# A hybrid decoder layer on one core: sample rows' output product on array quarters, the sample recurrence paused in each head's first group, weights on ScalarE's queue

## The chip, the cores and the metric

The kernel runs on one core of a Trainium2 chip. The core has TensorE (PE, a 128x128 array of multipliers; its weight loads are listed apart as PEld), VectorE (DVE), ScalarE (ACT), GpSimd (POOL) and SyncE (SP). SP computes nothing and issues most of the DMA transfers, in the order of its queue; ScalarE has a DMA queue too. The metric is the device time of one execution in microseconds. The times given are the median of several runs.

## The reference

One layer of a decoder works on 1024 prompt rows and on 32 sample rows (8 sequences of 4 new tokens), each of 1024 numbers:

```
h = x @ w_in                                     # 9344 columns
y_r = rwkv_mix(shifted columns, state)           # RWKV-7: 8 heads of 64, a recurrence over the tokens
y_a = merged dilated attention (3 groups x 4 heads x 128), softmax over the groups, times silu(gate)
mix = sigmoid(g_r) * (y_r @ w_oa) + sigmoid(g_a) * (y_a @ w_ob)
y   = layer_norm(ALPHA * x + mix @ w_out) * ln_g + ln_b
```

The outputs are `y` of the prompt and of the sample rows, the new keys and values, the new states of the recurrence and the last shifted row. Everything is fp32.

## The kernel before, in words

Tokens lie along columns: 1024 prompt tokens and 32 sample tokens make 1056 columns, worked in three chunks of 352 (`CH`). Large products are made of three products each (`mm3`, L171): operands are split into a high part and a rest (`hi`, `lo`, of type fp32r), and `hi*hi`, `lo*hi` and `hi*lo` are added up in PSUM. One chunk of one block of 128 output columns takes twelve products for 512 rows of the contraction.

The order of the work is written as a sequence of Python calls. A planner then lays out each engine's queue from it: by the written order first, but an instruction that is not ready in its model of the times can be passed by a later one. In stage one the order of TensorE is fixed by hand (`run_streams`); from there on the planner lays it out. Instructions given to `tc.keep_in_program_order` stay behind all that was written before them on their engine.

**Stage one** projects the shifted columns and the gates and runs the recurrence of the prompt. The change does not touch it.

**Attention** goes over four heads `h` and, in each, three groups `g`; n = 3h + g numbers these twelve steps. Each projects values, keys and queries (18 slots of twelve products) and between the slots works off a list `steps` of small closures that belong to the group before (`interleave`). So the closing work of head h is done among the projections of the next head's first group (g = 0). This closing work is of two kinds. `s_values` (`sv`) finishes the sample rows' attention: `pv0`, `pv1` and `pv2` multiply probabilities by cached values (L1093, on quarters of the array: the four sets of 32 output rows of the array, chosen by the partitions of the output), `pv2` then scales the result into `son` (L1113), and `out` transposes `son` on TensorE (L1118). `merge` (`me`) combines the three groups of the prompt's attention: `combine` computes weights and writes them to memory (`cd`), they come back spread over all partitions (`cb`, L1172), and `weight(0)`, `weight(1)`, `weight(2)` (L1177, L1180) and `last` (L1183) multiply and add 128x1024 tiles on VectorE.

The **sample recurrence** (`rec_step`, L760 to L767) is 16 steps of eight VectorE operations on 128x512 elements, 128 operations in all, with one GpSimd operation a step (L757). `interleave` calls `rec_some` after each slot, for one operation at a time, 18 a group. They are kept in program order. `rec_out` (L781 to L806), called at n = 10, stores the state, sends the outputs `oo` through memory (`od`, L782; back as `og` in tile `rtm`, L784), normalizes them on VectorE, transposes them (L798) and stores them for branch one.

**Branches.** `branch(0)` multiplies y_r by `w_oa`, `branch(1)` y_a by `w_ob`: 24 chunks each, eight blocks `d_` of three. Each chunk's gate `gt` (176 KB) is loaded by SP from `gd`, and VectorE multiplies PSUM by it: L1269 in branch one (in text: branch one is `b = 0`), L1266 in branch two, where GpSimd adds the result to `mix` (L1267). The first eight chunks of branch one run among the closing work of head 3. Beside branch two the rows of `w_out` are loaded into `xt` (three buffers, 512 KB each) and split into `wh` and `wl`.

**The last stage** (L1305) works off nine row blocks: eight of 128 prompt rows and one of the 32 sample rows. Each makes 48 products with 512 columns (L1323), adds the input (L1324), takes statistics (L1325, L1327), and normalizes: 704 columns (`CUT`) on VectorE, the other 320 with GpSimd's help.

Of the kernel before, what the change touches and what calls it, by code (L numbers as in the profile page):

```python
# [18 lines left out]
P = 128  # L19
D = 1024  # L20
# [25 lines left out]
def _constants():  # L46
# [17 lines left out]
    cst2 = np.concatenate([prev, cur, m3], 1)  # L64
# [18 lines left out]
def tile_layer(ctx: ExitStack, tc: tile.TileContext, A: dict, O: list):  # L83
# [72 lines left out]
    def load_w(src, n=4):  # L156
        raw = mk(wpool, [P, n, P], "wraw", 2)
        SP.dma_start(raw[:], src)
# [573 lines left out]
    SP.dma_start(cst2[:], A["cst2"])  # L732
# [325 lines left out]
    def s_values(h, Sa, sm):  # L1058
# [48 lines left out]
        def pv2():  # L1107
# [4 lines left out]
            for s_ in range(2):  # L1112
                V.tensor_scalar(on[:, s_], st["po"][s_][:, 0:P], sm[:, 5 + s_ : 6 + s_], None, ALU.mult)  # L1113
# [93 lines left out]
    for h in range(4):  # L1207
# [5 lines left out]
        for g in range(3):  # L1213
# [39 lines left out]
    def branch(b, hi, lo, w, mix):  # L1253
        cols = lambda d_: load_w(w[0, :, d_ * P : (d_ + 1) * P].rearrange("(k p) c -> p k c", p=P))
        ahead = cols(0)
        for d_ in range(8):
            wd, ahead = ahead, cols(d_ + 1) if d_ < 7 else None
            for c in range(3):
# [3 lines left out]
                gt = mk(stash, [P, CH], "gt", 3)  # L1262
# [15 lines left out]
    products = branch(0, yh, yl, A["w_oa"], mix)  # L1278
# [6 lines left out]
    for _ in products:  # L1285
        pass
# [3 lines left out]
    for n, _ in enumerate(branch(1, ah, al, A["w_ob"], mix)):  # L1290
        if n % 3 == 0:
            k = n // 3
# [7 lines left out]
    x_rows = lambda i: A["x_prompt"][0, i * P : (i + 1) * P, :] if i < 8 else A["x_sample"].rearrange("b t d -> (b t) d")  # L1300
    y_rows = lambda i: O[0][0, i * P : (i + 1) * P, :] if i < 8 else O[1].rearrange("b t d -> (b t) d")
    eps = mk(op, [P, 1], "eps")
    V.memset(eps[:], 16.0 * LN_EPS)
    CUT = 704
    for i in range(9):  # L1305
        n = P if i < 8 else NS
        sl = slice(i * P, i * P + n)
        mh, ml_ = (mk(op, [P, KT, P], t, 2, dt=F32R) for t in ("mh", "ml"))
        for h in range(2):
            k4 = slice(4 * h, 4 * h + 4)  # L1310
            split(mix[h][:, :, sl], mh[:, k4, 0:n], ml_[:, k4, 0:n])
        xt = mk(op, [P, D], "xt", 3)
        SP.dma_start(xt[0:n, :], x_rows(i))
        stt = mk(op, [P, 2, 6], "bst", 2)
# [48 lines left out]
```

## Time and profile before

| | |
|---|---|
| median of 3 runs | 1393.86 us (1392.2 to 1399.85) |
| profiled execution | 1398.63 us, its span 1396.8 us |
| TensorE products busy | 1354.3 us, 97% of the span |
| VectorE, ScalarE, GpSimd busy | 58%, 33%, 6% |
| mean granted TensorE clock | 0.993 |
| bytes moved by DMA | 151.29 MB, 108 GB/s on average |

The profile is one execution. Its span runs from the first to the last instruction on the core; the execution's own time is 1.8 us longer. In the timelines a row has the start and the length in us, the engine, the source line, the operation, output and inputs by name, the shapes, how many instructions were merged into the row, and in brackets the idle time before it with what ended it. A row of the waits gives engine, line, what was waited for, the total, how often, and the longest. In the groups the numbers behind the bar are busy us and mean ns of one, then the idle time before them.

### The profile page before, as it was taken

To read this page: it belongs to the slowest core of one execution; us is meant where nothing else is said; L and a number is where in the kernel's file an instruction comes from. 1 tells how busy PE (TensorE), PEld (TensorE's weight loads), DVE (VectorE), ACT (ScalarE), POOL (GpSimd) and SP (SyncE) were. 2 spreads that over 40 slices of the span, in tenths; PEclk is the share of its full clock that TensorE was granted. 3 is DMA by queue.
4 is the path that set the end of the run, shared out by engine and by line. 5 is a ranking of instruction groups with operands and counts; after the bars stand their busy time and mean duration, and the time that the engine had idled before them with its cause. 6 is when DMAs were issued, how large, how long until landed. Compare 5 with 4: busy or idle time off the path is not lost.

```text
span 1396.8 us, 25253 instructions
## 1 busy us (share of the span) xinstructions
PE 1354.3 (97%) x9765; PEld 1252.2 (90%) x9765; DVE 816.3 (58%) x2219; ACT 459.4 (33%) x1075; POOL 81.8 (6%) x92
## 2 busy tenths in 40 slices
PE   8999999999999999999999999999999999999997
PEld 7998989898988889999999899989998999898884
DVE  4358767586767767342555585548333524665675
ACT  4333434444344443422333223322323234132110
POOL 0000000000000000000000000000000000025122
PEclk9999999999999999999999999999999999999999
DMA  6212222312323233237544545555465556586121
GB/s 214 54 46 75 59 79 80 99 49 68 86 56 84 77 87 103 79 99 141 118 100 113 145 99 103 119 129 114 102 153 131 120 126 150 174 280 215 61 91 53
DMA packets 339742, 151.29 MB, mean 108 GB/s; under 512 B 188944, under 2 KB 329030, under 8 KB 339366
## 3 DMA queue, kind: packets, MB, share of 16 engines
q1 hardware_dynamic: 249190, 133.55, 35.0%
q10 hardware_dynamic: 90432, 16.13, 6.3%
q8 instruction: 77, 1.26, 0.4%
q14 instruction: 43, 0.35, 0.1%
HBM read 110.35 MB, written 38.97 MB: 107 GB/s over the span
## 4 chain that ended last, share of the span: by engine, by line
PE 76%; DVE 13%; DMA 6%; issue 2%; ACT 2%; POOL 0%; SPq 0%; DVEq 0%; ACTq 0%
PE pj L171 53%; PE pj L1323 7%; PE o L931 2%; PE s L894 2%; DVE tm L440 2%; DVE X L443 2%; DMA cb<-cd 2%; PE t L914 1%; PE s L1013 1%; PE sc L502 1%; DMA gt<-gd 1%; DVE wlo L162 1%; DMA cd<-nE 1%; PE g L369 1%; DVE st L510 1%
## 5 line engine op out<-in xcount | busy, mean ns | idle before, releaser
L171 PE MATMUL pj<-xhi,whi 128*128 128x352 f32 x1848 | 401.1, 338 | 4.3 <-DVE xlo L1269 2.0
L171 PE MATMUL pj<-xlo,whi 128*128 128x352 f32 x1848 | 384.0, 329 | 0.0
L171 PE MATMUL pj<-xhi,wlo 128*128 128x352 f32 x1848 | 382.8, 328 | 0.0
L171 PEld LDWEIGHTS pj<-xhi,whi 128*128 128x128 f32 x1848 | 304.8, 190 | 21.0 <-issue 10.4
L171 PEld LDWEIGHTS pj<-xhi,wlo 128*128 128x128 f32 x1848 | 309.3, 190 | 2.5 <-issue 0.8
L171 PEld LDWEIGHTS pj<-xlo,whi 128*128 128x128 f32 x1848 | 308.4, 190 | 2.9 <-issue 0.6
L162 DVE TENSOR_TENSOR wlo<-wraw,whi 128x512 fp32r<-128x512 f32 x162 | 113.1, 698 | 91.9 <-ACT whi L161 91.2
L161 ACT ACTIVATE whi<-wraw 128x512 fp32r<-128x512 f32 x162 | 100.7, 625 | 144.1 <-PE pj L171 71.5
L904 ACT ACTIVATE Sm<-Sm,nm 128x128 f32<-128x128 f32 (+1 forms) x96 | 42.4, 442 | 91.2 <-DVE nm L901 91.2
L510 DVE SCALAR_TENSOR_TENSOR st<-sc,E,SD 64x64 f32<-64x64 f32 x128 | 36.1, 282 | 47.3 <-PE sc L507 45.8
L1323 PE MATMUL pj<-wl,mh 128*128 128x512 f32 (+1 forms) x144 | 56.8, 394 | 0.0
L440 DVE TENSOR_TENSOR tm<-Y,X 128x60 f32<-128x60 f32 (+24 forms) x248 | 52.5, 212 | 6.3
L443 DVE TENSOR_TENSOR X<-X,tm 128x60 f32<-128x60 f32 (+24 forms) x248 | 51.9, 209 | 6.4
L896 DVE CUSTOM_DVE_ANT_0 Sm<-s,cst 128x128 f32<-128x128 f32 (+1 forms) x96 | 29.3, 346 | 41.4 <-PE s L894 41.3
L757 POOL TENSOR_TENSOR kvp<-vv,kv 128x512 f32<-128x512 f32 x16 | 21.1, 1324 | 406.4 <-DVE Ss L765 239.3
L493 ACT ACTIVATE SD<-st,E 128x128 f32<-128x128 f32 x64 | 25.6, 400 | 58.4 <-DVE st L510 58.4
L931 PE MATMUL o<-PT,Vt 128*128 128x128 f32 x280 | 38.7, 276 | 0.0
L819 ACT ACTIVATE k<-pj 128x352 f32<-128x352 f32 (+1 forms) x36 | 16.3, 454 | 66.2 <-PE pj L171 60.9
L894 PE MATMUL s<-k,q 128*128 128x128 f32 (+1 forms) x192 | 37.5, 325 | 0.0
L931 PEld LDWEIGHTS o<-PT,Vt 128*128 128x128 f32 x280 | 36.5, 191 | 0.4
L497 DVE TENSOR_TENSOR R<-sc,R 64x128 f32<-64x128 f32 x64 | 18.4, 288 | 30.4 <-PE sc L495 29.2
L502 PEld LDWEIGHTS sc<-R,AT 64*64 64x64 f32 x256 | 19.5, 133 | 18.1 <-DVE R L497 7.8
(295 smaller groups left out, 1753.9 us busy)
## 6 DMA issues: line engine op xcount, KB each, us to landing
wraw<-in_w_in_dram SPq DMA_DIRECT2D x146, 256.0 KB
gd<-zt SPq DMA_DIRECT2D x48, 176.0 KB
gt<-gd SPq DMA_DIRECT2D x48, 176.0 KB
vs<-bt ACTq DMA_DIRECT2D x48, 128.0 KB
kc<-in_cache_kv_g_dram SPq DMA_DIRECT2D x48, 128.0 KB
Vt<-vs ACTq DMA_DIRECT2D x12, 512.0 KB
cb<-cd SPq DMA_DIRECT2D x12, 512.0 KB
zd<-zt SPq DMA_DIRECT2D x24, 176.0 KB
```

The lines of the kernel that those rows point to most:

```text
L161: S.activation(hi[:], raw[:], AF.Copy)
L162: V.tensor_tensor(lo[:], raw[:], hi.bitcast(F32)[:], ALU.subtract)
L171: T.matmul(out, w[wi][:, n % 4, :], x[:, n % 4, :], start=first and n == 0, stop=last and n == 11)
L440: V.tensor_tensor(tm, Y[:, r : r + 1, r + 1 : 32].to_broadcast([P, m, n]), X[:, 0:m, r : r + 1].to_broadcast([P, m, n]), ALU.mult)
L443: V.tensor_tensor(X[:, 0:m, r + 1 : 32], X[:, 0:m, r + 1 : 32], tm, ALU.subtract)
L502: T.matmul(pu[u, 64 * e : 64 * e + 64], AT[u, e, c, u], R[u, 64 * e : 64 * e + 64], start=True, stop=True)
L510: V.scalar_tensor_tensor(S1[d, d], pS[d, d], E[d, c, 64:65], SD[d, d], ALU.mult, ALU.add)
L894: T.matmul(r, qT[:, i * P : (i + 1) * P], kT[:, keys[i][0] * P : keys[i][0] * P + n], start=True, stop=True)
L896: V.tensor_tensor_reduce(out=Sm[:, i, 0:n], in0=r, in1=m3 if g == 2 else m12[:, 256 - n : 256], scale=1.0, scalar=NEG, op0=ALU.add, op1=AL ...
L904: S.activation(Sm[:, i, 0:n], Sm[:, i, 0:n], AF.Exp, scale=SCALE, bias=nm[:, x : x + 1], accum_out=ml[:, g, 1, i : i + 1])
L931: T.matmul(po[:, (i % 4) * P : (i % 4 + 1) * P], st["Vt"][:, kb_, :], PT[:, n * P : (n + 1) * P], start=m == 0, stop=m == len(keys[i]) - 1,)
L1323: T.matmul(pb[0:n, :], a[:, k, 0:n], wk, start=x == 0, stop=x == len(prods) - 1)
```

## The change

1. **Sample rows.** The ninth row block of the last stage goes. Instead the sample rows' product with `w_out` is made beside branch two, in plain fp32 from the unsplit rows `raw` of `w_out`: for each of eight row blocks k of `w_out` one call of `sample_product(k)`, four products of 32 output rows and 256 columns, each on its own quarter of the array, added up in one PSUM tile `so`. It is called two blocks after `raw` was loaded, and k = 6 and 7 after the first row block of the last stage. `sample_norm` normalizes the result after the second row block: 32 rows of four quarters lie on 128 partitions, and two products with a constant matrix `quad` average over the four quarters. Its inputs are loaded late in branch two (`sample_loads`).
2. **Recurrence.** `rec_some` is called in groups with g > 0 only, where before it was called in all but the very first; what is left of the 128 operations is issued at n = 10, just ahead of `rec_out`.
3. **Closing work.** `son` is scaled on ScalarE instead of VectorE, and `out` comes behind `last` in the list.
4. **Weights of the branches** are issued on ScalarE's queue instead of SP's, two blocks ahead instead of one; `gt` has six buffers instead of three from the 19th chunk of branch one on.
5. **Last stage.** The normalization is written with fused operations, ScalarE does the scaling of the right part, GpSimd only one addition, `CUT` is 608, and in the last row block the second half of the columns is made in two products of 256 columns.

```diff
+    quad = np.where(i % 32 == j % 32, 0.25, 0.0)
+    cst2 = np.concatenate([prev, cur, m3, quad], 1)
...
-    def load_w(src, n=4):
+    def load_w(src, n=4, queue=SP):
         raw = mk(wpool, [P, n, P], "wraw", 2)
-        SP.dma_start(raw[:], src)
+        queue.dma_start(raw[:], src)
...
             for s_ in range(2):
-                V.tensor_scalar(on[:, s_], st["po"][s_][:, 0:P], sm[:, 5 + s_ : 6 + s_], None, ALU.mult)
+                S.activation(on[:, s_], st["po"][s_][:, 0:P], AF.Copy, scale=sm[:, 5 + s_ : 6 + s_])
...
-            ), 18, int(h + g > 0))
+            ), 18, int(g > 0))
             n = 3 * h + g
             if n == 10:
+                rec_some(8 * 4 * NT)
                 rec_out()
...
-                steps += [me[0], sv[1], me[1], sv[2], sv[3], me[2], sv[4], me[3], sv[5], sv[6], me[4], sv[7], me[5]]
+                steps += [me[0], sv[1], me[1], sv[2], sv[3], me[2], sv[4], me[3], sv[5], sv[6], me[4], me[5], sv[7]]
...
-    def branch(b, hi, lo, w, mix):
-        cols = lambda d_: load_w(w[0, :, d_ * P : (d_ + 1) * P].rearrange("(k p) c -> p k c", p=P))
-        ahead = cols(0)
+    def branch(b, hi, lo, w, mix, room):
+        cols = lambda d_: load_w(w[0, :, d_ * P : (d_ + 1) * P].rearrange("(k p) c -> p k c", p=P), queue=S) if d_ < 8 else None
+        ahead = [cols(0), cols(1)]
         for d_ in range(8):
-            wd, ahead = ahead, cols(d_ + 1) if d_ < 7 else None
+            wd = ahead.pop(0)
             for c in range(3):
...
+                if c == 0:
+                    ahead.append(cols(d_ + 2))
-                gt = mk(stash, [P, CH], "gt", 3)
+                gt = mk(room[0], [P, CH], "gt", room[1])
...
+    room = [stash, 3]
+    products = branch(0, yh, yl, A["w_oa"], mix, room)
...
+    for n, _ in enumerate(products):
+        if n == 10:
+            room[:] = op, 6
...
+    def sample_loads():
+        SP.dma_start(quad[:], A["cst2"][:, 384:512])
+        SP.dma_start(xs[:], A["x_sample"].rearrange("b t (x c) -> x (b t) c", x=4))
+        for x, ln in enumerate(("ln_g", "ln_b")):
+            SP.dma_start(lq[:, x], A[ln].rearrange("o (x c) -> x o c", x=4).to_broadcast([4, NS, 256]))
+    def sample_product(k):
+        for x in range(4):
+            T.matmul(
+                so[32 * x : 32 * x + 32, 0:256], mix[k // 4][:, k % 4, SEQ:TOK], raws[k][:, 256 * x : 256 * x + 256],
+                start=k == 0, stop=k == 7,
+            )
+    for n, _ in enumerate(branch(1, ah, al, A["w_ob"], mix, room)):
+        k = n // 3
         if n % 3 == 0:
             raw = mk(op, [P, D], "xt", 3)
+            raws.append(raw)
             SP.dma_start(raw[:], A["w_out"][0, k * P : (k + 1) * P, :])
             split(raw[:], wh[k // 4][:, k % 4, :], wl[:, k, :])
+        if n % 3 == 2 and k > 1:
+            sample_product(k - 2)
+        if n == 18:
+            sample_loads()
...
+    def sample_norm():
+        V.scalar_tensor_tensor(xs[:], xs[:], 4.0 * ALPHA, so[:, 0:256], ALU.mult, ALU.add)
...
+        T.matmul(so[:, 0:1], quad[:], mv[:, 0:1], start=True, stop=True)
...
+        T.matmul(so[:, 0:1], quad[:], mv[:, 1:2], start=True, stop=True)
...
-    CUT = 704
-    for i in range(9):
+    CUT = 608
+    for i in range(8):
...
+        parts = (0, 512, 1024) if i < 7 else (0, 512, 768, 1024)
...
+        if i == 0:
+            sample_product(6)
+            sample_product(7)
...
-        for eng, cs in ((G, slice(CUT, D)), (V, slice(0, CUT))):
-            xc = xt[0:n, cs]
-            V.tensor_scalar(xc, xc, mv[0:n, 0:1], mv[0:n, 2:3], ALU.subtract, ALU.mult)
-            eng.tensor_tensor(xc, xc, lng[0:n, cs], ALU.mult)
-            eng.tensor_tensor(xc, xc, lnb[0:n, cs], ALU.add)
-            SP.dma_start(y_rows(i)[:, cs], xc)
+        a, b = slice(CUT, D), slice(0, CUT)
+        V.scalar_tensor_tensor(xt[:, a], xt[:, a], mv[:, 0:1], lng[:, a], ALU.subtract, ALU.mult)
+        scale_of(mv)
+        S.activation(xt[:, a], xt[:, a], AF.Copy, scale=mv[:, 2:3])
+        G.tensor_tensor(xt[:, a], xt[:, a], lnb[:, a], ALU.add)
+        SP.dma_start(y_rows(i)[:, a], xt[:, a])
+        V.scalar_tensor_tensor(xt[:, b], xt[:, b], mv[:, 0:1], lng[:, b], ALU.subtract, ALU.mult)
+        V.scalar_tensor_tensor(xt[:, b], xt[:, b], mv[:, 2:3], lnb[:, b], ALU.mult, ALU.add)
+        SP.dma_start(y_rows(i)[:, b], xt[:, b])
+        if i == 1:
+            sample_norm()
```

More of the change, by code (lines that the diff above doesn't have):

```diff
@@ L1289, in tile_layer @@
     lng, lnb = mk(op, [P, D], "lng"), mk(op, [P, D], "lnb")
-    for n, _ in enumerate(branch(1, ah, al, A["w_ob"], mix)):
+    opsum = ctx.enter_context(tc.tile_pool(name="opsum", bufs=1, space=PSUM))
+    so = mk(opsum, [P, 512], "so")
+    xs = mk(op, [P, 256], "xs")
+    lq = mk(op, [P, 2, 256], "lq")
+    quad = mk(op, [P, P], "quad")
+    def sample_loads():
[3 more added lines that the diff above has]
+            SP.dma_start(lq[:, x], A[ln].rearrange("o (x c) -> x o c", x=4).to_broadcast([4, NS, 256]))
```

52 lines of the change are left out of this document (30 added, 22 removed).

## The prediction

> **What bounds the kernel now.** I read the page first, then the waits of TensorE, then a table by stretch around each wait, then the timelines at those places.
>
> ```profile
> span 1396.8 us, 25253 instructions
> PE 1354.3 (97%) x9765; PEld 1252.2 (90%) x9765; DVE 816.3 (58%) x2219; ACT 459.4 (33%) x1075; POOL 81.8 (6%) x92
> ```
>
> TensorE is the bound. An edit pays only if it takes products away, takes a wait of TensorE away, or shortens what follows its last product. The waits that stand in the region of the change:
>
> ```profile
> PE t L1118 <- DVE son L1113: 8.8, 4, 3.4
> ...
> PE pj L171 <- DVE gt L1266: 3.9, 4, 1.2
> ...
> PE pj L171 <- ACT whi L161: 1.7, 2, 1.4
> ```
>
> Behind the three long waits for `son` the granted clock falls (columns: stretch, length, then busy time and instructions of PE, PEld, DVE, ACT, POOL, then PE clock, DMA share, GB/s):
>
> ```profile
> 802.47:809.29 6.82, 5.53 (x20) 5.49 (x21) 6.67 (x10) 0.00 (x0) 0.00 (x0) 0.50 0.35 77
> 942.41:945.83 3.42, 3.42 (x13) 3.35 (x14) 3.35 (x5) 0.00 (x0) 0.00 (x0) 0.50 0.48 155
> 1082.36:1085.77 3.41, 3.41 (x13) 3.41 (x12) 3.41 (x5) 0.00 (x0) 0.00 (x0) 0.50 0.63 174
> 809.29:812.70 3.41, 3.41 (x23) 3.36 (x22) 3.41 (x6) 0.00 (x0) 1.04 (x1) 1.00 0.39 137
> ```
>
> At full clock 3.41 us hold 23 products, at 0.50 only 13. So each short stretch loses 3.41 x (1 - 13/23) = 1.5 us; the long one holds 20 products in 5.53 busy us, worth 20/23 x 3.41 = 3.0, and loses 2.6. That is 5.5 us on top of the 8.8 waited: the `son` waits cost 14.3 us.
>
> Why `son` is late, at head 0 (the timelines of PE, of DVE and of ACT):
>
> ```profile
> 795.80 0.40 PE L1093 MATMUL s<-c,KT 76*32 76x128 f32 x8
> ...
> 797.50 0.80 PE L171 MATMUL pj<-xlo,whi 128*128 128x352 f32 x4
> 798.13 0.80 PE L171 MATMUL pj<-xhi,whi 128*128 128x352 f32 x4
> ...
> 803.76 0.47 PE L1118 MATMUL t<-ident,son 128*128 128x128 f32 x1 [3.40 <-DVE son L1113]
> ```
> ```profile
> 796.62 1.23 DVE L1177 TENSOR_TENSOR o<-o,cb 128x1024 f32<-128x1024 f32 x1 [2.92 <-DMA cb<-cd]
> 797.77 0.68 DVE L761 TENSOR_REDUCE sa<-rtm 128x8 f32<-128x512 f32 x1
> 798.36 2.00 DVE L1177 TENSOR_TENSOR o<-o,cb 128x1024 f32<-128x1024 f32 x1
> ...
> 800.87 1.97 DVE L1180 TENSOR_TENSOR o<-o,o 128x1024 f32<-128x1024 f32 x1
> ...
> 803.60 0.36 DVE L1113 TENSOR_SCALAR son<-s,sm 128x128 f32<-128x128 f32 x1
> ```
> ```profile
> 798.33 0.44 ACT L819 ACTIVATE q<-pj 128x320 f32<-128x320 f32 x1 [2.21 <-PE pj L171]
> ```
>
> The products that `son` scales were done at 796.2. VectorE stood at the head of its queue waiting for `cb` until 796.62, then did two merge weights and recurrence operations, and reached the second `son` at 803.60. TensorE had asked for it at 803.76 - 3.40 = 800.4.
>
> **The change part by part.**
>
> *`son` on ScalarE, `me[5]` ahead of `out`, recurrence paused.* ScalarE is idle for 2.2 us before the eviction of `q` at 798.33 (0.44 us for 320 columns); two scalings of 128 columns fit ahead of it or behind it, before 800.4. So 14.3 us are free to go. Late next is VectorE itself: the merge still starts when `cb` lands. The tightest weights afterwards:
>
> ```profile
> 826.31 0.81 DVE L162 TENSOR_TENSOR wlo<-wraw,whi 128x512 fp32r<-128x512 f32 x1
> ```
> ```profile
> 827.57 0.81 PE L171 MATMUL pj<-xhi,wlo 128*128 128x352 f32 x4
> ```
>
> They are ready at 827.12 and used at 827.57: 0.45 us to spare. TensorE would now come 3.4 + 2.6 = 6.0 us earlier; VectorE loses the two `son` scalings (0.6) and the five recurrence operations of the paused group that ran between 797 and 811 (0.7 each, as the 0.68 above), 4.1 us. So a new wait of 6.0 - 4.1 - 0.45 = 1.5 us at head 0. At heads 1 and 2 TensorE comes about 3.3 us earlier (a third of the other 5.4 us waited, and 1.5 of clock): less than the 4.1 at head 1, so 0; at head 2 no recurrence ran before, and up to ten of group ten's operations (7 us) now stand there: 2.5, between 0 and 7. Gain 14.3 - 4 = 10.3; bounds 14.3 (nothing late next) and 2 (VectorE as late as TensorE is early, with the clock falling again).
>
> The Trainium skill, TensorE: Matmul & The Clock Gate, Part 1, says that the clock halves after an idle window of about 3.4 us. The rows go further: waits shorter than 3.4 us were followed by it as well. By the rule only the first wait's 2.6 us would be credited and the sum would end 2.9 us higher.
>
> *The recurrence later.* It ends with group ten, where before it had ended in group eight. What hangs on it:
>
> ```profile
> 1034.07 0.53 SPq L782 DMA_DIRECT2D od<-oo x1
> ...
> 1039.45 0.33 SPq L784 DMA_DIRECT2D rtm<-od x1
> ```
> ```profile
> 1127.75 0.43 PE L798 MATMUL t<-ident,rtm 32*128 32x32 f32 x4
> ```
>
> The chain store, reload (5.4 us), eight or more VectorE operations, transposes had 88 us to spare before its transposes; now it starts near them. An order made by a planner can move the transposes behind group eleven's products; if it reckons a landing too short (the merge's `cb` came 2.9 us later than the queue was laid out for), VectorE stands still twice that, 5.8 us. I take +1.5 between 0 and 7.3 (5.8 and one clock stretch), nearer to the row in which the transposes waited for nothing.
>
> *Weights on ScalarE's queue, two ahead; `gt` six deep.* What they can win is 3.9 (`gt`) and the two waits for `whi`, 1.7: 5 us or a little more, nearly all in branch two.
>
> ```profile
> 1220.00:1287.00 67.00, 62.07 (x372) 59.91 (x373) 42.58 (x60) 19.22 (x24) 24.79 (x22) 1.00 0.81 258
> ```
>
> The DMA engines are busy 81% there, and the same bytes in 5 us less would need 87%. So not all of it comes: -3, between -5 and 0. ScalarE is busy 19 of 67 us, so sixteen issues cost nothing on it; without that cover they would be 16 x 0.38 = 6 us:
>
> ```profile
> 1263.46 0.38 SPq L158 DMA_DIRECT2D wraw<-in_w_ob_dram  x1
> ```
>
>  Queued behind such an issue is the next activation on ScalarE, but the buffer that it waits for is freed a block before.
>
> The Trainium skill, DMA: Bandwidth & Descriptors, Issuing engines are not separate DMA queues, holds that transfers of all issuing engines share the same 16 DMA engines. By it the queue change alone brings nothing; the depth would have to. No run here shows the queue by itself yet.
>
> *Sample rows' product.* Gone is the ninth row block; its first and last products:
>
> ```profile
> 1376.63 0.40 PE L1323 MATMUL pj<-xhi,mh 128*32 128x512 f32 x1
> ...
> 1387.46 0.39 PE L1323 MATMUL pj<-wl,mh 128*32 128x512 f32 x1
> ```
>
> 48 products, (1387.46 - 1376.63)/47 = 0.230 us apart: 11.1 us of TensorE, without a gap. Instead come 32 fp32 products with 256 columns on quarters, four at a time. The nearest rows:
>
> ```profile
> 729.42 0.64 PE L171 MATMUL pj<-xlo,whi 128*128 128x352 f32 x3
> 729.99 0.63 PE L1013 MATMUL s<-KT,qS 128*32 128x256 f32 x4
> 730.54 0.92 PE L171 MATMUL pj<-xhi,whi 128*128 128x352 f32 x4
> ...
> 785.20 0.43 PE L1093 MATMUL o<-kc,KT 128*32 128x128 f32 x8
> 785.56 0.74 PE L171 MATMUL pj<-xhi,whi 128*128 128x352 f32 x3
> ```
>
> A product is two records. Two quarters with 256 columns hold the array 0.55 us; four quarters with 128 columns 0.36, so four lie beside each other. On entering, the last `L171` product (the third, at 729.74) holds 0.25 instead of the 0.16 that the rows of head 0 give ((798.13 - 797.50)/4). So a set of four is 0.55 + 0.09 = 0.64, eight sets 5.2. Net -5.9. Bounds: -11 if the sets fall wholly into waits of branch two, +6.6 if the quarters run one after another (32 at 24.3/44 = 0.55, as two records of the first row below, a full-array product with 256 columns).
>
> ```profile
> L894 PE MATMUL s<-k,q 128*128 128x256 f32 x88 | 24.3, 380 | 0.0
> ...
> L312 PE MATMUL g<-cst,t 128*128 128x2 f32 x64 | 7.8, 244 | 0.0
> ```
> ```profile
> L1266 DVE SCALAR_TENSOR_TENSOR gt<-gt,pj 128x352 f32<-128x352 f32 x24 | 12.3, 515 | 11.6 <-DMA gt<-gd 10.8 <-PE pj L171 0.7
> ```
> ```profile
> L1324 DVE SCALAR_TENSOR_TENSOR xt<-xt,pj 128x512 f32<-128x512 f32 x16 | 10.9, 683 | 27.2 <-PE pj L1323 27.2
> L1334 POOL TENSOR_TENSOR xt<-xt,lnb 128x320 f32<-128x320 f32 x8 | 10.7, 1340 | 0.6
> ```
>
> The two small `quad` products (0.24 each by the second row) and a short wait for VectorE: +0.7, between 0.4 and 3. The split of the last 512 columns into two of 256: 24 more products; from 0.160 at 352 and 0.230 at 512 columns I get 0.118 at 256, 48 x 0.118 = 5.7 against 24 x 0.230 = 5.5: +0.2; if a product of 256 columns took as long as one of 352, 48 x 0.160 = 7.7, +2.2.
>
> *The end.*
>
> ```profile
> 1387.85:1396.80 8.95, 0.00 (x0) 0.00 (x0) 5.55 (x8) 0.29 (x1) 2.58 (x2) 0.79 0.06 15
> ```
> ```profile
> 1393.31 1.07 SPq L1335 DMA_DIRECT2D out_dram<-xt  x2
> ```
>
> After the last product 8.95 us pass, 2.4 of them after the last store's issue (1394.38). New, from 515 ns at 352 and 683 at 512 columns on VectorE: 0.41 each for the evacuation and the statistics of 256 columns and 0.58 for 416; 0.4 for the aggregate and the reciprocal, an estimate as two tiny operations at less than a third of the 683; 0.44 x 416/320 = 0.57 on ScalarE; 1340 x 416/320 = 1740 ns on POOL; 0.4 for hand-overs: 4.5. Then the issue, 0.3, the 2.4, and 0.8 for a last store of 311 KB instead of 90 KB (221 KB at the 258 GB/s of branch two): 8.0 in all, -0.9, between -2 and +0.5. The VectorE and POOL work of the seven blocks before stays under TensorE's 11.2 us a block.
>
> **The sum.** -10.3 + 1.5 - 3 - 5.9 + 0.7 + 0.2 - 0.9 = -17.7. The profiled execution took 1398.63 (span 1396.8 and 1.8 around it): 1380.9. That execution lies 4.8 above the median of the three times, 1393.86, from which the same sum gives 1376.2. I cannot tell how much of those 4.8 us is the clock that the change restores, and take a value between: **1378**, with 1367 to 1385 as its own range.
>
> **The rivals.**
>
> *VectorE takes the place of `son`* (same place, next wait). For: the 0.45 us above, and a merge that starts with a landing. Against: the paused recurrence. It would leave 2 of the 14.3 us: 8.3 above the sum, **1386**.
>
> *The sample recurrence comes too late.* 5.8 us of waiting and a clock stretch of 1.5 in group eleven, against 1.5 in the sum: 5.8 above, **1384**. For: 88 us of slack gone. Against: nothing of group eleven needs its result, so the transposes can stand later in TensorE's order.
>
> *Quarters one after another.* 17.7 us instead of 5.2: **1390**. Against it stands the row with eight records in 0.36 us.
>
> *Slower: the raw rows hold the loads.* The sample product reads the unsplit rows of `w_out`, so each of the three `xt` buffers is held until the end of the block after next, and row k+3 can be loaded only then. SP issues in order: `gt` loads behind it wait as well. If five such loads each stall TensorE for 3.4 us, its longest wait now, and halve the clock for one stretch (1.5), 24 us return: **1402**. It decides from about 3 us a block, clock included. Against: `gt` is six deep, six sets of twelve products (1.9 us each) ahead, and its longest wait for `gt` with three was 1.2.
>
> **How the numbers follow.** The forecast 0.60; VectorE next 0.14; recurrence late 0.11; quarters 0.05; raw rows 0.04; better than 1367, with the sets hidden and all waits gone, 0.06. What a measurement of this kernel can tell from no change is about 0.5%, 7 us: faster means below 1386.9. The forecast and the better case give 0.65 of their 0.66, the recurrence rival 0.09 of its 0.11, VectorE's 0.08 of its 0.14, the quarters 0.01 of 0.05: faster 0.83. What they leave, 0.01 + 0.02 + 0.06 + 0.04, is the same: 0.13. Slower 0.04. The range 1364 to 1390 leaves out the slower case and the tails.
>
> **What would show it.** Right: no row `L1118 <- son`, clock 1.00 through the three places, at most 2 us waits for `wlo` or `s` near them; sets of eight records in branch two with 0.55 us to the next product; last product at about 1370 in the span and 8 us behind it. Wrong: waits of PE for L798 or for `gt` in branch two, sets of 2 us, or a new clock stretch at 0.50 in a head's first group.

## The result and the profile after

The changed kernel takes 1380.83 us (median of four, 1379.83 to 1381.54); the kernel before, timed beside it, 1396.86 us. The ratio is 0.9884, 95% interval 0.9842 to 0.9925: faster by 1.2%. The profiled execution took 1381.54 us, with a span of 1379.8 us, 17.0 less than the span before.

The head of the page after, and then its waits of TensorE (engine, line, what was waited for, total us, times, longest):

```profile
span 1379.8 us, 25342 instructions
PE 1344.1 (97%) x9809; PEld 1245.0 (90%) x9809; DVE 804.0 (58%) x2203; ACT 467.2 (34%) x1089; POOL 67.2 (5%) x82
```

```profile
PE pj L172 <- ACT xhi L1245: 3.0, 1, 3.0
...
PE s L1094 <- DMA kc<-in_cache_kv_g_dram: 2.1, 2, 1.2
PE s L895 <- DVE ml L897: 1.6, 2, 0.9
PE pj L172 <- ACT whi L162: 1.3, 1, 1.3
PE t L799 <- DVE rtm L796: 0.9, 1, 0.9
```

The waits for `son` (8.8 us) and for `gt` (3.9) are gone. At the top of this region stands a wait that was not there before: 3.0 us for `xhi`, in branch one. (The wait for `whi` is at 29 us, in stage one, and was there before: 1.35 of the 1.7 us that the prediction counted for branch two.)

To see where 17.0 us come from, I cut both spans at the same places of the program: from group three to group eleven; group eleven; branch one; branch two; the last stage up to its last product; the end. Columns: stretch, length, busy us of the five engines, clock, DMA share, GB/s. First the kernel before:

```profile
752.42:1128.11 375.69, 367.40 (x2644) 346.56 (x2642) 198.15 (x474) 111.84 (x303) 15.06 (x11) 0.98 0.53 120
1128.11:1173.02 44.91, 44.91 (x289) 41.83 (x287) 16.88 (x44) 15.82 (x38) 1.68 (x3) 1.00 0.61 148
1173.02:1234.33 61.31, 58.08 (x470) 54.74 (x467) 35.79 (x81) 16.54 (x40) 0.00 (x0) 1.00 0.60 177
1234.33:1287.03 52.70, 48.26 (x288) 46.35 (x289) 33.46 (x45) 14.77 (x19) 24.82 (x22) 1.00 0.80 257
1287.03:1387.85 100.82, 100.81 (x434) 77.22 (x432) 64.64 (x100) 12.24 (x25) 22.61 (x19) 1.00 0.21 72
```

The changed kernel, with the end as well:

```profile
752.75:1116.09 363.34, 361.61 (x2641) 340.67 (x2639) 191.28 (x449) 113.21 (x307) 12.59 (x10) 1.00 0.53 121
1116.09:1162.33 46.24, 45.36 (x292) 42.01 (x291) 21.98 (x60) 16.29 (x38) 2.73 (x4) 1.00 0.60 138
1162.33:1229.08 66.75, 59.96 (x469) 55.86 (x467) 40.53 (x86) 19.52 (x46) 0.00 (x0) 0.97 0.80 237
1229.08:1280.17 51.09, 51.09 (x338) 47.29 (x337) 30.28 (x41) 14.02 (x18) 25.49 (x23) 1.00 0.60 179
1280.17:1371.74 91.57, 91.57 (x432) 74.18 (x428) 53.74 (x92) 15.11 (x28) 10.45 (x9) 1.00 0.25 88
1371.74:1379.75 8.01, 0.00 (x0) 0.00 (x0) 4.28 (x7) 0.94 (x2) 1.06 (x1) 0.69 0.18 66
```

Row by row: the heads give 12.35 us, group eleven costs 1.33 and branch one 5.44, branch two gives 1.61 although the sample rows' sets are now in it, the last stage gives 9.25 and the end 0.94. Together that is 17.4; group three starts 0.3 us later than before. So the gain after the heads is partly paid back in branch one.

What happens in branch one of the changed kernel, in the timelines of SP's queue, of ScalarE and of TensorE:

```profile
1143.23 0.36 SPq L807 DMA_DIRECT2D yd<-yS  x1
...
1165.11 8.50 SPq L1074 DMA_DIRECT2D c<-kvn  x12
1173.70 0.39 SPq L1252 DMA_DIRECT2D cb<-yd  x1
```
```profile
1176.06 0.31 ACT L1245 ACTIVATE xhi<-cb 128x128 fp32r<-128x128 f32 x1 [2.03 <-DMA cb<-yd]
```
```profile
1172.23 1.16 PE L932 MATMUL o<-PT,Vt 128*128 128x128 f32 x8 [0.85 <-ACT PT L919]
1176.42 0.95 PE L172 MATMUL pj<-xhi,whi 128*128 128x352 f32 x3 [3.03 <-ACT xhi L1245]
```
```profile
1176.80:1180.21 3.41, 3.41 (x20) 2.85 (x18) 2.10 (x10) 0.24 (x1) 0.00 (x0) 0.50 0.64 170
```

The sample rows' 32 columns of y were stored at 1143. Their chunk is the last that branch one reads back, and it is issued at 1173.70, behind twelve small copies of new values into a cache tile, 8.5 us of SP's queue. TensorE waits 3.03 us for its split, and then runs one stretch of 3.41 us at half clock, which by the prediction's count loses 1.5 us. All waits of TensorE in branch one add up to 6.7 us, two for `kc` (2.1) among them, where the kernel before had 3.1; with the clock that is 5.1 of the 5.4 us. In the kernel before, that chunk was issued 2.3 us ahead of the same store and copies:

```profile
1173.97 0.37 SPq L1250 DMA_DIRECT2D cb<-yd  x1
...
1176.23 2.13 SPq L1069 DMA_DIRECT2D out_dram<-kvn  x3
```

### The profile page after: what moved, and what is told of

Its sections match the earlier page's. It is cut to its first block, busy times and chain, and to the rows that moved or that the text cites. A ratio compares the mean times of both kernels' runs of the same rounds, so it can differ in the third digit from the quotient of the medians.

```text
span 1379.8 us, 25342 instructions
## 1 busy us (share of the span) xinstructions
PE 1344.1 (97%) x9809; PEld 1245.0 (90%) x9809; DVE 804.0 (58%) x2203; ACT 467.2 (34%) x1089; POOL 67.2 (5%) x82
## 4 chain that ended last, share of the span: by engine, by line
PE 74%; DVE 14%; DMA 7%; issue 2%; ACT 2%; SPq 1%; DVEq 0%; ACTq 0%
PE pj L172 52%; PE pj L1378 7%; DVE tm L441 2%; DVE X L444 2%; PE o L932 2%; DMA cb<-cd 2%; PE s L895 2%; DMA wraw<-in_w_in_dram 1%; DVE wlo L163 1%; DVE o L1178 1%; PE t L915 1%; PE sc L503 1%; PE s L1014 1%; PE g L370 1%; DVE AT L377 1%
## 5 line engine op out<-in xcount | busy, mean ns | idle before, releaser
L1378 PE MATMUL pj<-wl,mh 128*128 128x512 f32 (+1 forms) x136 | 52.0, 382 | 0.0
L299 ACT ACTIVATE zt<-pj,der 128x352 f32<-128x352 f32 x48 | 26.4, 551 | 27.9 <-PE pj L172 26.7
```

Of the source, the lines that this page charges most:

```text
L1378: T.matmul(pb[:], a[:, k], wk, start=x == 0, stop=x == len(prods) - 1)
```

## The experiments

Every edit is made to the changed kernel. The planner lays out the order of all engines anew for each, so an edit also moves instructions that it does not name. To see where a run's time went, the table has three lengths of its profiled execution: the heads (group three to eleven), then group eleven with branch one, then branch two up to the last stage's first product, each cut at the first product of the next part. "Half clock" is the time at 0.50 in the first two.

| kernel | time, us (range) | heads | group 11 and branch one | branch two | half clock |
|---|---|---|---|---|---|
| before (profile above) | 1396.86 | 375.7 | 106.2 | 52.7 | 13.7, 0 |
| changed (profile above) | 1380.83 (1379.83–1381.54) | 363.3 | 113.0 | 51.1 | 0, 3.4 |
| changed, repeated | 1380.69 (1377.75–1383.57) | 361.4 | 112.9 | 51.1 | 0, 6.8 |
| recurrence unpaused | 1387.67 (1386.02–1391.16) | 374.3 | 108.6 | 51.1 | 10.2, 3.4 |
| `son` on VectorE | 1388.07 (1386.39–1390.53) | 371.0 | 114.6 | 51.1 | 6.8, 6.8 |
| sample y direct | 1384.30 (1383.98–1387.05) | 361.9 | 118.0 | 51.1 | 0, 17.1 |
| copies on GpSimd | 1374.43 (1374.25–1374.83) | 363.3 | 106.7 | 52.8 | 0, 0 |
| weights on SyncE | 1379.19 (1379.04–1379.84) | 362.9 | 111.6 | 51.1 | 0, 3.4 |
| sample y direct, weights on SyncE | 1377.17 (1376.45–1377.87) | 362.2 | 112.1 | 51.1 | 0, 6.8 |
| recurrence early | 1375.24 (1374.52–1378.15) | 364.3 | 107.5 | 51.1 | 0, 0 |
| loads undone | 1379.77 (1379.11–1381.60) | 363.7 | 110.9 | 53.0 | 0, 0 |
| copies on GpSimd, recurrence early | 1376.94 (1376.49–1378.75) | 364.2 | 106.8 | 52.4 | 0, 3.4 |
| the same, gates on GpSimd | 1385.46 (1384.37–1390.92) | 365.4 | 113.5 | 53.1 | 3.4, 10.2 |

The kernel before took 1396.7 us beside the first group of runs (from the repeat to "sample y direct"), 1397.6 beside the second (to "recurrence early") and 1397.5 beside the third.

**The changed kernel once more.** No edit; it anchors the others.

> The changed kernel once more, as the yardstick of the three that run beside it on the same chip: 1380 to 1382 us. TensorE waits 3.0 us for the sample rows' chunk of y at the start of branch one, and the clock halves for 3.4 us behind it.

1380.69 us, ratio to before 0.9868 (0.9835 to 0.9902). The wait in branch one is there again, 3.2 us, with two stretches of half clock.

**The recurrence's pauses undone.** The recurrence runs in all groups but the first again, as before.

```diff
-            ), 18, int(g > 0))
+            ), 18, int(h + g > 0))
```

> Undoes the pause alone: the sample recurrence runs in every group but the first again and ends in group eight. Theory (the pause, by making the recurrence end late, put the load of the sample rows' y behind twelve small copies on SP): the 3.0 us wait in branch one and the slow stretch behind it are gone, -4.5 us there; in the heads VectorE does 18 operations of 0.69 us more in the first group and TensorE waits 1 to 3 us more at each of two heads. Together 1376 to 1382. Rival (TensorE merely arrives at branch one ten us earlier than before, the pause has nothing to do with it): the wait stays, the heads lose as well, 1383 to 1388.

1387.67 us, ratio 0.9924 (0.9897 to 0.9952): the rival's number. The largest wait of TensorE:

```profile
PE s L895 <- DVE ml L897: 8.5, 2, 4.3
```

The heads lose 11 to 13 us against the two profiles of the changed kernel: VectorE is late with the softmax of a head's first group, 4.3 us twice, and the clock halves behind it. With `son` on ScalarE alone, VectorE is simply late at the next thing. The forecast had 1 to 3 us at each of two heads.

The wait for `xhi` in branch one is gone here, and group eleven with branch one is 4.3 us shorter: the pause buys the heads and is paid for there. But the theory's reason is wrong. The chunk still stands behind the copies on SP's queue:

```profile
1172.84 8.70 SPq L1074 DMA_DIRECT2D c<-kvn  x12
1181.64 0.39 SPq L1252 DMA_DIRECT2D cb<-yd  x1
```

It is issued 11.6 us after branch one's start, against 11.4 in the changed kernel. So the pause did not put it there; what differs is that TensorE has other products in that place (the run with the recurrence early, below, shows them).

**`son` back on VectorE.** The pauses stay.

```diff
-                S.activation(on[:, s_], st["po"][s_][:, 0:P], AF.Copy, scale=sm[:, 5 + s_ : 6 + s_])
+                V.tensor_scalar(on[:, s_], st["po"][s_][:, 0:P], sm[:, 5 + s_ : 6 + s_], None, ALU.mult)
```

> Undoes the move of son to ScalarE alone. Theory (son was late because it stood behind the merge's weights on VectorE): with the recurrence paused son still comes behind two weights, so TensorE waits 1 to 2.5 us for it at three heads and the clock halves behind some of these: +4 to +10 us, 1385 to 1391. Rival (the pause of the recurrence is what freed son): +1 at most, 1381 to 1382.

1388.07 us, ratio 0.9929 (0.9901 to 0.9956), as the theory said.

```profile
PE t L1119 <- DVE son L1114: 6.3, 3, 2.3
```

The heads take 371.0 us. With 375.7 before, the pauses alone have won 4.7 there; `son` alone won 1.4 (375.7 to 374.3, the run above); both together 12.4. The two edits are worth twice as much together as one by one; with either alone TensorE still has waits in the heads behind which the clock halves (6.8 and 10.2 us of it in the table). The heads of the two profiles of the changed kernel differ by 1.9 us, so the 1.4 is not clear of that; and all three keep the new order of the closing work (`out` behind `last`), which no run undoes.

**Sample rows' y split straight from its tile.** The store of the sample rows' y to memory and its load back are left out.

```diff
-        SP.dma_start(yd[0:4, :, SEQ:TOK].rearrange("j p t -> p j t"), yS[:])
+        rec["y"] = yS
...
-            raw = stage()[:, :, 0:m]
-            SP.dma_start(raw, yd[4 * b : 4 * b + 4, :, t0 : t0 + m].rearrange("k p t -> p k t"))
+            if b == 0 and t0 == SEQ:
+                raw = rec["y"][:]
+            else:
+                raw = stage()[:, :, 0:m]
+                SP.dma_start(raw, yd[4 * b : 4 * b + 4, :, t0 : t0 + m].rearrange("k p t -> p k t"))
```

> The sample rows' y for branch one is split straight from its tile in SBUF; its store to memory and its load back are left out, nothing else changes. Theory: the 3.0 us wait for that load and the slow stretch behind it (1.5 us lost) go: 1375.5 to 1377. Rival (branch one is held by the head's merge and weights anyway, and the wait moves on): 1379.5 to 1381.

1384.30 us, ratio 0.9900 (0.9863 to 0.9937): slower than either theory allowed. The awaited chunk is gone, and so is the wait for it; the group eleven and branch one part grew to 118.0 us. Its timelines of TensorE, VectorE and ScalarE say why:

```profile
1184.17 1.54 PE L172 MATMUL pj<-xhi,whi 128*128 128x352 f32 x4 [3.63 <-DVE xhi L1276]
```
```profile
1183.00 0.69 DVE L163 TENSOR_TENSOR wlo<-wraw,whi 128x512 fp32r<-128x512 f32 x1 [1.56 <-ACT whi L162]
1183.61 0.51 DVE L1276 SCALAR_TENSOR_TENSOR xhi<-gt,pj 128x352 f32<-128x352 f32 x1
```
```profile
1172.03 0.37 ACTq L159 DMA_DIRECT2D wraw<-in_w_oa_dram  x1
...
1179.06 0.60 ACT L937 ACTIVATE o<-o 128x512 f32<-128x512 f32 x1 [5.66 <-PE o L932]
...
1179.56 0.38 ACTq L159 DMA_DIRECT2D wraw<-in_w_oa_dram  x1
...
1182.34 0.63 ACT L162 ACTIVATE whi<-wraw 128x512 fp32r<-128x512 f32 x1 [1.62 <-DMA wraw<-in_w_oa_dram]
```

Read it backwards. TensorE waits for a product's PSUM, which VectorE frees with the row that starts at 1183.61; ahead of that on VectorE stands the split of a weight; that waits for ScalarE's split, that for the weight's landing; and the load was issued only at 1179.56, on ScalarE's queue, right behind the scaling of `o`, before which ScalarE stood 5.66 us. VectorE also waits 3.3 and 6.3 us for gates (`gt`) later in that stage. So I formed a second theory: branch one is set by what stands in order behind something that waits, on whichever engine. Four runs test it.

**The small copies on GpSimd's queue**, in the last head only.

```diff
-                    SP.dma_start(c[64 + 4 * g + t : 65 + 4 * g + t], kvn[32 * g + t : 32 * g + 32 : NT, 1, :])
+                    (G if h == 3 else SP).dma_start(c[64 + 4 * g + t : 65 + 4 * g + t], kvn[32 * g + t : 32 * g + 32 : NT, 1, :])
```

> The twelve small copies of the last head's new keys and values (the group c<-kvn) are issued by GpSimd, which is idle from 1143 to the end of branch one in the changed kernel, and no longer by SyncE. Theory: the 3.0 us wait of branch one and the half clock after it come from SyncE's order alone, the sample rows' chunk being issued at 1173.70 behind 8.5 us of these copies. Then the wait for xhi and the clock drop are gone, branch one falls from some 67 us to 61 to 63, and the time is 1374 to 1378 us, some 4 below the changed kernel. Rival: the chunk is not what sets branch one (VectorE's and ScalarE's order do, as the run without the store and load had it with 72 us of branch one): the time is 1380 us or more, with a new wait of TensorE of 3 us or more in branch one.

1374.43 us, ratio 0.9838 (0.9815 to 0.9862): the theory, and the fastest kernel of this study, 0.45% under the changed one; their ranges do not meet, though they were timed in two groups of runs. Timelines of SP's queue, GpSimd and ScalarE:

```profile
1163.43 0.77 SPq L1252 DMA_DIRECT2D cb<-yd  x1
```
```profile
1161.68 6.31 POOL L1074 DMA_DIRECT2D c<-kvn  x12 [20.27 <-DMA out_dram<-Vt]
```
```profile
1166.13 0.31 ACT L1245 ACTIVATE xhi<-cb 128x128 fp32r<-128x128 f32 x1 [3.81 <-DMA cb<-yd]
```

The chunk is issued and split 10 us earlier, and no stretch of half clock is left before the end. GpSimd had nothing else to do there. Branch one takes 60.2 us, a little under the forecast's 61 to 63, though 2.9 us of waits for gated products remain; branch two is 1.7 us longer than in the changed kernel.

**The branch weights on SyncE's queue.**

```diff
-        cols = lambda d_: load_w(w[0, :, d_ * P : (d_ + 1) * P].rearrange("(k p) c -> p k c", p=P), queue=S) if d_ < 8 else None
+        cols = lambda d_: load_w(w[0, :, d_ * P : (d_ + 1) * P].rearrange("(k p) c -> p k c", p=P), queue=SP) if d_ < 8 else None
```

> The branch weights are loaded from SyncE's queue again, two ahead as in the changed kernel; nothing else differs. Theory: the queue alone is worth nothing in branch two, because the weights are asked for two sets ahead: 1379 to 1382.5 us, and branch two still without waits. Rival one: ScalarE's queue was what ended branch two's waits; on SyncE's queue they return, some 5 us: 1384 to 1387. Rival two: ScalarE's own waits hold the weights of branch one back, so that SyncE's queue is better there by 2 to 3 us: 1377 to 1379.

1379.19 us, ratio 0.9874 (0.9845 to 0.9902), within the theory, and branch two is the same 51.1 us without a wait. The rule that the prediction weighed (the Trainium skill, DMA: Bandwidth & Descriptors, Issuing engines are not separate DMA queues) agrees with it for these sixteen large loads. In branch one the chunk now goes ahead of the copies (1162.27 against 1165.74), but another wait, 4.5 us for a product's PSUM, has come. So the nearly equal time is the balance of two different orders, and the queue's own worth there can't be read from it.

The chunk's place follows this queue in every profile that has the chunk and the copies on SP: ahead of the copies where SP issues the branch weights (the kernel before, this run, and "loads undone" below), behind them where ScalarE does (the changed kernel and its repeat, the recurrence unpaused, `son` on VectorE, the recurrence early). So the late chunk comes with part 4 of the change, not with the pauses.

**Both: sample y direct, and the weights on SyncE's queue.** The same store and load are left out.

> As the run in which the sample rows' y is split straight from its tile (its store to memory and the load back left out), with the branch weights on SyncE's queue as well. Theory: in that run a weight load of branch one was issued at 1179.56, seven microseconds after the one before it, because it stood on ScalarE's queue behind a ScalarE instruction that waited for TensorE; VectorE's split of that weight then stood in front of the gated products and TensorE waited 3.6 us, and the half clock followed. On SyncE's queue that is gone: branch one 61 to 65 us instead of 72, time 1375 to 1379. Rival: the gate loads behind SyncE's own waits do it, whichever queue holds the weights: branch one 68 us or more, 1381 to 1386.

1377.17 us, ratio 0.9858 (0.9834 to 0.9882): 7 us below the run with the weights on ScalarE's queue, as the theory said of the time and of the wait of 3.6 us, which is gone. Branch one by itself is 65.8 instead of 72.4 us, a little above the expected range and the same as in the run before (65.7): a wait of 4.6 us with two stretches of half clock remains. The theory's step is not shown, though: the load in question is issued at 1178.34 on SyncE's queue, only 1.2 us earlier. What differs is VectorE's order, which has three gated products at 1178.49 to 1180.06, ahead of that weight's split at 1184.59.

**The recurrence early.** Two steps for one in group one; the pauses stay.

```diff
-            ), 18, int(g > 0))
+            ), 18, int(g > 0) + int(h == 0 and g == 1))
```

> The sample recurrence takes two steps instead of one behind each product of group one (head one's second group), so that of its 128 steps 126 are done before group ten instead of 108; the pauses in the first groups stay. Theory: the recurrence's lateness costs what it does in group eleven (0.9 us of wait) and nothing in branch one, whose wait is SyncE's order: 1378.5 to 1381.5 us. Rival one: the lateness is what pushes the sample rows' chunk behind the copies; with it gone the wait of 3.0 us and the half clock go, as without the pauses, and the time is 1374 to 1378. Rival two: VectorE is too full in group one, waits of some 4 us come back there: 1383 to 1386.

1375.24 us, ratio 0.9848 (0.9822 to 0.9874): the first rival's number, but not quite its story. The chunk is issued as late as ever behind the copies (SP's queue and ScalarE):

```profile
1162.93 8.45 SPq L1074 DMA_DIRECT2D c<-kvn  x12
1171.47 0.39 SPq L1252 DMA_DIRECT2D cb<-yd  x1
```
```profile
1176.00 0.30 ACT L1245 ACTIVATE xhi<-cb 128x128 fp32r<-128x128 f32 x1
```

Only TensorE doesn't wait for it, because the planner has set other products in that place:

```profile
1172.91 1.04 PE L1083 MATMUL t<-ident,Sa 128*128 128x128 f32 x8
1174.14 0.62 PE L1094 MATMUL o<-kc,KT 128*32 128x128 f32 x10 [0.19 <-ACT KT L1088]
...
1176.16 0.33 PE L1119 MATMUL t<-ident,son 128*128 128x128 f32 x1 [0.48 <-ACT son L1114]
1176.35 0.92 PE L172 MATMUL pj<-xhi,whi 128*128 128x352 f32 x4
```

In the changed kernel these products of the sample rows' attention came later (L1083 at 1185.76, L1094 from 1188.67 on). The unpaused run has the same rows in the same order there, from 1184.11 on. So what the recurrence's lateness costs is the cover: products that would have run while the chunk is under way.

**The loads undone.** Weights from SyncE's queue, one set ahead, three `gt` buffers at a time (from the 19th chunk of branch one on still three others than before it).

```diff
-        cols = lambda d_: load_w(w[0, :, d_ * P : (d_ + 1) * P].rearrange("(k p) c -> p k c", p=P), queue=S) if d_ < 8 else None
-        ahead = [cols(0), cols(1)]
+        cols = lambda d_: load_w(w[0, :, d_ * P : (d_ + 1) * P].rearrange("(k p) c -> p k c", p=P), queue=SP) if d_ < 8 else None
+        ahead = [cols(0)]
         for d_ in range(8):
             wd = ahead.pop(0)
+            ahead.append(cols(d_ + 1))
...
-                if c == 0:
-                    ahead.append(cols(d_ + 2))
...
-            room[:] = op, 6
+            room[:] = op, 3
```

> The branch loads as in the kernel before: the weights from SyncE's queue, one set ahead, and three gate buffers in both branches; all the rest as in the changed kernel. Theory: the depth of the loads (two sets ahead, six gate buffers) is what ended branch two's waits. Undone, they return: branch two's products from the first to the last take 55 to 57 us instead of 50.3 (before: 52.5 without the sample products' 4.0), and the time is 1384 to 1387 us beside 1380.7 of the changed kernel. Rival: the waits went because the planner placed the other loads (gamma, beta, the first rows of the output weights) ahead of branch two, whatever the depth: 1378.5 to 1382 us and branch two as short as in the changed kernel.

1379.77 us, ratio 0.9871 (0.9855 to 0.9888): the same as the changed kernel. From the first to the last product branch two takes 52.2 us, against 50.3; I had expected 55 to 57. Depth, with the queue, is worth 1.9 us there, and in this run the waits of branch one were spread so that none halved the clock, which gives as much back. Of the waits for `gt` 1.6 us are back. The rest of what branch two gained did not come from these edits. What the rows above show in its place is traffic: the DMA share fell from 0.80 to 0.60 in branch two (13.5 MB to 9.1) and rose from 0.60 to 0.80 in branch one. In this run branch two moves 11.8 MB; three loads of prompt rows for the last stage, 512 KB each, that the kernel before issued there are issued there neither in this run nor in the changed kernel. That this is the cause is near the rival's story, and it is argued, not tested by itself.

**Copies on GpSimd and the early recurrence together**, both edits as above.

> The small copies of the last head on GpSimd's queue and the recurrence's two steps for one in group one, together. Theory: both runs took away the same cost, the branch-one wait with its half clock (6.3 and 5.5 us each), so together they bring little more than one: 1373 to 1375.5 us. Rival: the costs are different ones (the wait behind the copies in the one, the recurrence's lateness in group eleven and the products placed by it in the other), and add: 1368 to 1371 us. Third: the planner's new order brings a wait of its own, 1376 us or more.

1376.94 us, ratio 0.9855 (0.9840 to 0.9870): the third case. They do not add; a wait for `kc`, 1.9 us, has come in branch one, with one stretch of half clock. Branch two is 1.3 us longer than in the changed kernel, as it was, by 1.7, with the copies alone.

**Branch one's gate loads on GpSimd's queue too.** Added to the run above.

```diff
-                SP.dma_start(gt[:], gd[8 * b + d_, :, sl])
+                (SP if b else G).dma_start(gt[:], gd[8 * b + d_, :, sl])
```

> As the run with the copies on GpSimd's queue and the early recurrence, with branch one's gate loads on GpSimd's queue too. Theory: what is left of branch one's waits (2.9 us in the run with the copies alone, on the gated product's PSUM) comes from gate loads that stand on SyncE's queue behind merge loads which wait; without that branch one is below 60 us and the time 1.5 to 3 us under the run with both. Rival: VectorE's own order (the merge's sums of 2 us in front of the gated products) sets them: within 1 us of the run with both.

1385.46 us, ratio 0.9922 (0.9898 to 0.9945): 8.5 us slower than without it, which neither theory held. TensorE waits 3.4 us for `kc` and 2.3 for a gated product, with 10.2 us at half clock in branch one and 3.4 in the heads. Why `kc` lands late there I did not follow; it stays open.

## Why the prediction was right, and where it was not

The time came out 2.8 us above the forecast and inside its own narrow range. The sum of the steps was -17.7 against the profiled execution; the profiled spans differ by 17.0. That the sum came so near is luck: the heads gave 2.1 and the branch loads 3.2 us more than forecast, the later recurrence cost 5.3 more and the sample product gave 0.7 less.

*Heads: -10.3 forecast, -12.4 measured.* The mechanism held: no wait for `son`, clock 1.00 from group three to eleven. "Late next is VectorE itself" held too, but the residual was 1.6 us of waits for `ml` instead of 4, and no stretch of half clock. Undoing the pause alone gives back 11 us or more, so the credit of the paused operations, which was my reason against the rival "VectorE takes the place of `son`", was the step that carried this. The rival is what the kernel does without the pauses.

*Recurrence later: +1.5 forecast, +6.8 measured in group eleven and branch one.* This is the step that failed, in size and in place. Group eleven paid what I took, 1.33 us, with 0.9 us of wait at the transposes. I looked only at who waits for the result itself, and wrote "nothing of group eleven needs its result". But branch one does, through a store, a reload and a split, and it grew by 5.4 us. Two things met there. The chunk stands behind the copies, which comes with the weights on ScalarE's queue, a part for which the sum had only a gain. And the products that could cover it had moved, which comes with the late recurrence. The rival's price, 5.8 and a clock stretch, 7.3 in all, was nearly the right amount; its place was one stage too early. With the early recurrence this part goes from 113.0 to 107.5, unpaused to 108.6, with the copies moved away to 106.7, with 106.2 before: restoring the cover or clearing the queue is enough. It is not the whole account, since in the two runs where the weights' queue alone put the chunk ahead of the copies, the part still takes 111.6 and 110.9 us with other waits; why those come stays open.

*Branch loads: -3 forecast, -6.2 measured.* The stage fell by 1.6 while six sets of the sample product, 0.77 each, came into it. In the kernel before, the 288 products of branch two take 6.3 us more than 288 times 0.161; in the changed kernel nothing is left over beside the sets. The waits on record there were 4.2 us, not 5.6, as one wait for `whi` belongs to stage one; the rest are products beside the waits that start 0.24 to 0.44 us apart instead of 0.16. The reason that I gave against a full win, 81% busy DMA engines, fell: the share in branch two dropped to 0.60. Of the 6.2 only 1.9 come from the loads' depth and queue; the cause of the rest is open.

*Sample product: -5.9 forecast, -5.2 measured.* The timeline of TensorE:

```profile
1252.49 0.81 PE L172 MATMUL pj<-al,whi 128*128 128x352 f32 x4
1253.23 0.64 PE L1313 MATMUL so<-xt,xhi 128*32 128x256 f32 x8
1253.80 0.92 PE L172 MATMUL pj<-ah,whi 128*128 128x352 f32 x4
```

From the start of the first of eight records to the next product 0.57 us, 0.09 more on entering, as reckoned (0.74 instead of 0.65 for the four products ahead), and 0.11 more on leaving, which the term lacked (0.92 instead of 0.81 for the four behind). That is 0.77 for each of six sets, and 1.2 for the pair made after row block zero: 5.8 against 11.1 of the ninth row block. (Eight sets at the reckoned 0.64 are 5.1, not the 5.2 of the prediction.) The quarters run beside each other, so that rival is out; the slower rival too, as TensorE waited for no `gt` in branch two.

*The split of the last 512 columns and the end.* The first and the last of 48 products of 256 columns, and the last store's issue, in the timeline:

```profile
1365.89 0.28 PE L1378 MATMUL pj<-xhi,mh 128*128 128x256 f32 x1
...
1371.46 0.28 PE L1378 MATMUL pj<-wl,mh 128*128 128x256 f32 x1
...
1376.22 0.33 SPq L1394 DMA_DIRECT2D out_dram<-xt  x1
```

(1371.46 - 1365.89)/47 = 0.1185 us, as reckoned. The end took 8.01 us, reckoned 8.0, which is partly luck: the reckoned path went through GpSimd's addition, which was shorter than estimated (1.06 against 1.74 us) and let its store go at 1375.57. The path that ended last is VectorE's left part, 0.84 and 1.72 us on 608 columns, which the sum did not have; its store went at 1376.22. The two `quad` products cost 0.14 each and 0.08 more at the product behind: 0.44 in all, instead of 0.7 with a wait that did not come.

*The base.* Against its own profiled execution the sum gave 1380.9. I took 2.9 off because that execution lay above the median of the three times shown. With the later runs the median of the kernel before is 1396.7 to 1397.6, between the two bases and nearer to the profiled one. From 1397 the same sum gives 1379.3: about half of the 2.8 us is the base, the other half the sum.

## What to carry to other kernels

When a step is made later, follow its result through every store, reload and queue up to the product that finally reads it; the wait may stand a stage away from where the step ends, and it takes two things, what stands ahead of the load in its queue and what the waiting engine has left to do meanwhile. Before a time is taken as proof of a mechanism, check that the row which the mechanism names has moved: in three runs here the time or the end of a wait came out as a theory had it, and the load that it named had hardly moved. Two edits against one engine's lateness are to be priced together, since half a cure still leaves waits that halve the clock. Under a planner, a change of one order is a change of all: read the new order before crediting a gain, and do not add the gains of two runs.

## What the runs showed of the hardware

**The clock is decided on a fixed grid, and about half a window of idleness is enough.** In each of the eleven profiles that have more than one stretch of half clock, all begin at whole multiples of 3.413 us from one another; in the changed kernel 302.99 and 1176.80 are 256 of them apart. I laid that grid over each of the thirteen profiles and took from the product records how long TensorE was idle in each window, up to the last product. Of some 5140 windows at full clock, 18 had 1.91 us or more idle, and each of the 18 was followed by half clock. The next longest idle time, 1.76 us, was not. Of the windows under that, eight were followed by half clock, with 0.07 to 1.67 us idle; all eight hold products on part of the array or of few columns, but so do about a thousand others that were not, and I have no explanation for these. So it matters where a wait falls. In the run with copies and early recurrence a wait of 1.94 us lies whole in one window (the windows of that run on its grid):

```profile
1185.82:1189.23 3.41, 1.48 (x16) 0.99 (x15) 1.12 (x2) 0.41 (x2) 0.00 (x0) 1.00 0.93 269
1189.23:1192.64 3.41, 3.41 (x24) 2.58 (x25) 0.00 (x0) 0.37 (x1) 0.00 (x0) 0.50 0.63 173
```

In the run with the early recurrence alone a longer one, 2.46 us, is split over two windows and costs no clock:

```profile
1076.05:1079.46 3.41, 2.33 (x15) 2.04 (x13) 3.34 (x3) 0.00 (x0) 0.00 (x0) 1.00 0.49 78
1079.46:1082.87 3.41, 2.03 (x11) 1.93 (x12) 2.36 (x11) 1.68 (x6) 0.00 (x0) 1.00 0.50 155
```

The Trainium skill, TensorE: Matmul & The Clock Gate, Part 1, gives the window as 3413 ns and free-running, which these traces bear out; its condition for the slow state, an idle window, is too strict by them, and the prediction read it as one wait of 3.4 us.

**What issuing a small copy costs its queue.** Twelve copies of eight rows took 8.5 us of SyncE's queue, 0.71 each, and 6.31 us on GpSimd, 0.53 each. The Trainium skill, DMA: Bandwidth & Descriptors, Issuing engines are not separate DMA queues, says that issuing from several engines saves the issuing time alone, usually small beside the transfer. Here the run that moved it off the one queue was 6.3 us faster (1380.7 to 1374.4).
